# Seven products of quarter sums in place of eight quarter products: the up product of a two-layer hybrid model on one Trainium2 core

## The chip, the core and the metric

The kernel runs on one core of a Trainium2 chip. A core has a tensor engine (TensorE, in the profile PE for its matmuls and PEld for its weight loads), a vector engine (VectorE, DVE), a scalar engine (ScalarE, ACT), GpSimd (POOL) and SyncE (SP), which here issues nearly all transfers between DRAM and the on-chip memory SBUF. Each engine works its own list of instructions in order and waits on the others by semaphores; matmul results lie in PSUM, which DVE and ACT read. The metric is the device time of one execution in microseconds.

## What is computed

The model has two layers, width 1024, 1024 tokens, hidden width 2816, everything in float32. The change concerns the feed-forward part, `conv_ffn`, once in each layer:

```python
def rms_norm(x, gain):
    xf = x.astype(jnp.float32)
    y = xf * lax.rsqrt(jnp.mean(xf * xf, axis=-1, keepdims=True) + EPS)
    return (y * gain.astype(jnp.float32)).astype(x.dtype)

def conv_ffn(x, w_up, conv_w, conv_b, w_down):
    hid = causal_dwconv(x @ w_up, conv_w, conv_b)
    gate, val = jnp.split(hid, 2, axis=-1)
    return (jax.nn.gelu(gate) * val) @ w_down

def reference(...):
    for l in range(DEPTH):                        # DEPTH = 2
        h = rms_norm(x, g[0])
        if l % 2 == 0:
            ...                                   # recurrent mixers: hgrn2_mix and rglru_mix, then even_w_out
        else:
            ...                                   # fox_attention over 16 heads, then odd_w_out
        x = x + rms_norm(mix, g[1])
        h = rms_norm(x, g[2])
        x = x + rms_norm(conv_ffn(h, ffn_w_up[l], ffn_conv_w[l], ffn_conv_b[l], ffn_w_down[l]), g[3])
    return x
```

`x @ w_up` gives 2 × 2816 columns (gate and val), the convolution runs over three tokens of each column, and the gated product goes through `w_down`. In the terms of the kernel a column block of 128 is a *f* (22 of them, for gate and val), a block of 128 input channels is a *k* (8), and the tokens are two *halves* of 512.

## The kernel before

**Exact products.** A float32 operand is split in two: its leading 12 bits (a cast on ACT, L153 or L158) and the exact rest (a subtraction on DVE, L154 or L159; on POOL while `low[0]` is set). Each product of 128 × 128 by 128 × 512 is three matmuls, `mm3` (L161 to L164): lead by lead, lead by rest, rest by lead.

**Weights.** `load_split` fetches a piece of 128 × 512 by SP into one of three buffers (`rawp`, tile `raw`), casts it and subtracts. The split goes into one of four buffers `hl` (`wp`), or, for the pieces of `w_down` that half 1 keeps (`wk`), into room of its own. The raw buffer is free again when the subtraction is done.

**Up.** `ffn` runs over the halves, in each over f, in each over gate and val. `proj_cols` makes 8 k × 3 matmuls into a PSUM bank `pj`; ACT scales and adds the bias (L371), DVE adds the two earlier tokens out of PSUM (L376), with the last two columns of half 0 kept in `halo` (L381, L386); then gelu on ACT (L389), the product of gate and val on DVE (L390), and the split into the tile `act`, which stays in SBUF for down. So up of a half is followed by down of the same half, and `w_up` is fetched twice in each layer.

**Down and out.** `tok_proj` is a product with tokens on the PSUM partitions: for the first 512 output columns it goes over all k, in each fetching a weight piece and making 4 token tiles × 3 matmuls, then again for the second 512 columns (in passes over token tiles, `passes`). Half 1 of down has the callback `beside=keep`, which during the first columns also fetches and keeps the second columns' weights of the first 8 k (layer 0) or 16 k (layer 1). The norm of the result, the residual and the norm of the next stage follow on ACT and DVE (`squares` L296, `gains` L300, residual L338, `norm_rows` L230 and L236). The normed rows are transposed on PE and split (`turn`); `turn_later` sets after how many product steps that is done, by `NORM_STEPS`, so that other products stand between.

**Order.** PE's order is the order of the program (from layer 0's out product on it is fixed by hand); the lists of ACT, DVE, POOL and SP are set by a scheduler when the kernel is built. On all of them an instruction that waits holds up everything behind it.

## Time and profile before

Three runs took 2567.44 us in the median (2566.65 to 2569.66). The profiled execution has a span of 2567.0 us.

| | busy us | share | instructions |
|---|---|---|---|
| PE | 2489.4 | 97% | 11790 |
| DVE | 1658.2 | 65% | 3440 |
| ACT | 1190.4 | 46% | 2234 |
| POOL | 214.3 | 8% | 187 |

251.39 MB of transfers went at 98 GB/s in the mean. Up takes about 440 to 690 and 830 to 1070 us in layer 0, 1830 to 2080 and 2200 to 2440 us in layer 1; down follows each of them.

A row of a group reads: line, engine, operation, written tile<-read tiles, shapes, xcount | busy us, mean ns of one | idle us of the engine just before, and what ended most of it. A row of a timeline reads: start, duration, engine, line, operation, [idle before <-what released it]. A row of waits reads: who waits <- for whom: us in total, times, longest.

### The profile page before, as it was taken

To read this page: it belongs to the slowest core of one execution; us is meant where nothing else is said; L and a number is where in the kernel's file an instruction comes from. 1 tells how busy PE (TensorE), PEld (TensorE's weight loads), DVE (VectorE), ACT (ScalarE), POOL (GpSimd) and SP (SyncE) were. 2 spreads that over 40 slices of the span, in tenths; PEclk is the share of its full clock that TensorE was granted. 3 is DMA by queue.
4 is the path that set the end of the run, shared out by engine and by line. 5 is a ranking of instruction groups with operands and counts; after the bars stand their busy time and mean duration, and the time that the engine had idled before them with its cause. 6 is when DMAs were issued, how large, how long until landed. Compare 5 with 4: busy or idle time off the path is not lost.

```text
span 2567.0 us, 33472 instructions
## 1 busy us (share of the span) xinstructions
PE 2489.4 (97%) x11790; PEld 2050.7 (80%) x11790; DVE 1658.2 (65%) x3440; ACT 1190.4 (46%) x2234; POOL 214.3 (8%) x187
## 2 busy tenths in 40 slices
PE   8999999999999999999989999989899999999998
PEld 6887787788887788887778888877788888788887
DVE  5677766866524766636788888886766642666643
ACT  5333754544423444434556565664544432344441
POOL 2000001200001100000111111132300000300000
PEclk9999999999999999999999999999999999999999
DMA  4111125333334333335221222125433332533343
GB/s 133 33 42 34 47 90 181 124 96 98 99 97 138 98 96 97 125 110 162 69 51 45 53 56 52 51 89 188 159 91 98 96 99 99 156 99 95 101 160 112
DMA packets 131833, 251.39 MB, mean 98 GB/s; under 512 B 16112, under 2 KB 21520, under 8 KB 131664
## 3 DMA queue, kind: packets, MB, share of 16 engines
q1 hardware_dynamic: 129792, 244.34, 31.0%
q0 software_dynamic: 1440, 4.38, 0.7%
q8 instruction: 93, 1.52, 0.2%
q14 instruction: 76, 0.62, 0.1%
q10 hardware_dynamic: 432, 0.53, 0.1%
HBM read 219.23 MB, written 21.56 MB: 94 GB/s over the span
## 4 chain that ended last, share of the span: by engine, by line
PE 78%; DVE 14%; ACT 3%; DMA 2%; issue 2%; POOL 0%; SPq 0%; DVEq 0%; ACTq 0%; POOLq 0%
PE pj L162 15%; PE pj L163 15%; PE pj L164 15%; PE dn L162 7%; PE dn L163 7%; PE dn L164 7%; DVE nm L1003 2%; ACT pl L1013 2%; PE py L162 1%; DVE pt L159 1%; PE py L164 1%; PE py L163 1%; DVE lg L1001 1%; DVE y L338 1%; DVE ht L236 1%
## 5 line engine op out<-in xcount | busy, mean ns | idle before, releaser
L162 PE MATMUL pj<-hh,hl 128*128 128x512 f32 x1952 | 781.3, 400 | 18.1 <-DVE cv L381 9.2
L164 PE MATMUL pj<-hh,hl 128*128 128x512 f32 x1952 | 764.4, 392 | 0.9 <-POOL hl L154 0.8
L163 PE MATMUL pj<-hl,hl 128*128 128x512 f32 x1952 | 764.3, 392 | 0.0
L153 ACT CAST hl<-raw 128x512 fp32r<-128x512 f32 x687 | 423.5, 618 | 624.7 <-PE dn L164 319.8
L154 DVE TENSOR_TENSOR hl<-raw,hl 128x512 fp32r<-128x512 f32 x567 | 391.6, 692 | 371.5 <-ACT hl L153 371.0
L162 PEld LDWEIGHTS pj<-hh,hl 128*128 128x128 f32 x1952 | 368.9, 189 | 87.3 <-issue 20.1
L164 PEld LDWEIGHTS pj<-hh,hl 128*128 128x128 f32 x1952 | 368.0, 189 | 81.0 <-POOL hl L154 2.2
L376 DVE SCALAR_TENSOR_TENSOR cv<-pj,cw,cv 128x511 f32<-128x511 f32 x352 | 262.6, 746 | 251.3 <-ACT cv L371 251.3
L163 PEld LDWEIGHTS pj<-hl,hl 128*128 128x128 f32 x1952 | 369.3, 189 | 65.4 <-issue 0.2
L154 POOL TENSOR_TENSOR hl<-raw,hl 128x512 fp32r<-128x512 f32 x120 | 163.5, 1367 | 1244.2 <-ACT hl L153 1218.5
L371 ACT ACTIVATE cv<-pj,cw 128x512 f32<-128x512 f32 x176 | 137.3, 780 | 219.8 <-PE pj L164 219.6
L163 PE MATMUL dn<-hl,act 128*128 128x512 f32 x608 | 236.5, 389 | 0.0
L162 PE MATMUL dn<-hl,act 128*128 128x512 f32 x608 | 236.5, 389 | 0.0
L164 PE MATMUL dn<-hl,act 128*128 128x512 f32 x608 | 236.5, 389 | 0.0
L164 PEld LDWEIGHTS dn<-hl,act 128*128 128x128 f32 x608 | 114.1, 188 | 23.8
L162 PEld LDWEIGHTS dn<-hl,act 128*128 128x128 f32 x608 | 114.1, 188 | 23.6
L163 PEld LDWEIGHTS dn<-hl,act 128*128 128x128 f32 x608 | 114.1, 188 | 23.6
L158 ACT CAST pt<-tr 128x512 fp32r<-128x512 f32 (+1 forms) x160 | 86.8, 543 | 51.0 <-PE tr L1031 50.1
L1003 DVE TENSOR_REDUCE nm<-lg 128x1 f32<-128x512 f32 (+2 forms) x192 | 105.4, 553 | 4.6 <-PE lg L999 1.0
L159 DVE TENSOR_TENSOR pt<-tr,pt 128x512 fp32r<-128x512 f32 (+1 forms) x160 | 100.9, 633 | 7.9 <-ACT pt L158 6.3
L1013 ACT ACTIVATE pl<-lg,nm 128x512 f32<-128x512 f32 (+3 forms) x128 | 76.7, 605 | 43.9 <-DVE nm L1011 41.1
L1047 PE MATMUL o<-pt,v 128*128 128x256 f32 x320 | 77.5, 309 | 14.1 <-DVE pt L159 10.3
(323 smaller groups left out, 3354.4 us busy)
## 6 DMA issues: line engine op xcount, KB each, us to landing
raw<-in_w_up_dram SPq DMA_DIRECT2D x352, 256.0 KB
raw<-in_w_down_dram SPq DMA_DIRECT2D x202, 256.0 KB
raw<-in_w_out_dram SPq DMA_DIRECT2D x71, 256.0 KB
mid<-y SPq DMA_DIRECT2D x24, 512.0 KB
xt<-mid SPq DMA_DIRECT2D x24, 512.0 KB
raw<-in_w_qkv_dram SPq DMA_DIRECT2D x48, 256.0 KB
raw<-in_w_mix_dram SPq DMA_DIRECT2D x40, 256.0 KB
xr<-in_x_cols_dram SPq DMA_DIRECT2D x16, 256.0 KB
```

Source lines behind the costliest of these rows:

```text
L153: act.copy(hl[:, 0], raw)
L154: (pool if low[0] else dve).tensor_tensor(out=hl[:, 1], in0=raw, in1=hl[:, 0].bitcast(F32), op=ALU.subtract)
L158: act.copy(hi, src)
L159: dve.tensor_tensor(out=lo, in0=src, in1=hi.bitcast(F32), op=ALU.subtract)
L162: pe.matmul(o, wh, xh, start=start, stop=False)
L163: pe.matmul(o, wh, xl, start=False, stop=False)
L164: pe.matmul(o, wl, xh, start=False, stop=stop)
L371: act.activation(out=y, in_=u, func=AF.Identity, scale=cw[:, 2, c : c + 1], bias=cw[:, 3, c : c + 1])
L376: dve.scalar_tensor_tensor(out=y[:, d:], in0=u[:, : HT - d], scalar=wcol, in1=y[:, d:], op0=ALU.mult, op1=ALU.add,)
L1003: dve.tensor_reduce(out=nm[:, x0 : x0 + 1], in_=lg[:, :n], axis=AX.X, op=ALU.max, negate=True)
L1013: act.activation(out=p[:, cs], in_=lg[:, :n], func=AF.Exp, bias=nm[:, 0:1], accum_out=sm[:, x0 : x0 + 1])
L1047: pe.matmul(o, v[:, kb, :], pt[s][:, 0:256], start=(u == 0 and s == 0), stop=False, skip_group_check=True,)
```

## The change

The up product of both halves is made as a two-by-two block product in the form of Strassen and Winograd. With the weights as blocks a11, a12 (gate; the two halves of the input channels) and a21, a22 (val), and the activations as b11, b21 (half 0) and b12, b22 (half 1), the four results need seven products of quarter size:

- P1 = a11·b11, a12·b21, s2·t2, s1·t1, s3·t3, s4·b22, a22·t4;
- s1 = a21 + a22, s2 = s1 − a11, s3 = a11 − a21, s4 = a12 − s2;
- t1 = b12 − b11, t2 = b22 − t1, t3 = b22 − b12, t4 = the difference of b21 and t2.

Each is 4 k × 3 matmuls. `up(l, hb)` holds the whole stage for both halves:

- The normed rows are now only copied after the transpose, in float32 (`hb`, one tile per half); the sums are formed in float32 and then split. Half 0's b11 and b21 are split first.
- For the first three f (`AHEAD`) the two products P1 and a12·b21 need half 0 alone. They are made while half 1 is still being normed and turned, and their sums are written to DRAM (`started`) and fetched back in the loop.
- The operands t2, t1, t3, b22, t4 are then formed and split: the differences on DVE and POOL, the splits on ACT and DVE (t4's rest on POOL).
- In the loop over f POOL and DVE form s1 to s4, the splits follow; the products add up in two PSUM banks `y` and `z`, with copies of P1, u2 and q kept in SBUF (`tap`). The sums c1 (gate) and c2 (val) lie in SBUF over all 1024 tokens, so that the convolution runs over 1024 at once without `halo`.
- The gated product of a f, 512 KB, is written to DRAM (`hidden`). Down fetches it again, 128 × 512 for each k of each half, through the raw ring, casts and subtracts (`fetch`, up to three k ahead).
- `w_up` is fetched once in each layer. The pools are opened by stage (`open_stage`, `open_rows`). Layer 0's out product of half 1 runs its second columns in two passes of two token tiles; `NORM_STEPS` of half 1 is (27, 20) in place of (36, 46). A gain vector of layer 1 is loaded when first used.

```diff
--- before.py
+++ after.py
...
-NORM_STEPS, DOWN_NORM_STEPS, TURN_STEPS = (36, 46), (32, 42), 2
+NORM_STEPS, DOWN_NORM_STEPS, TURN_STEPS = ((36, 46), (27, 20)), (32, 42), 2
+AHEAD = 3
...
+    pools = {}
+    stage = [None]
+    def open_stage(**bufs):
+        if stage[0] is not None:
+            stage[0].close()
+        stage[0] = ExitStack()
+        pools.clear()
+        for name, n in bufs.items():
+            pools[name] = stage[0].enter_context(tc.tile_pool(name=name, bufs=n, reuse_waits="tile"))
+    def open_rows():
+        open_stage(s4=NSLOT, s2=NHALF)
+    open_rows()
...
+    hidden = [
+        [dram.tile([P, T], F32, tag=f"hid{l}_{f}", name=f"hid{l}_{f}") for f in range(FT)]
+        for l in range(2)
+    ]
+    started = [dram.tile([P, 2, HT], F32, tag=f"started{f}", name=f"started{f}") for f in range(AHEAD)]
...
-            hh, hl = h[t // 4]
             c0 = (t % 4) * P
             tp = tr()
             for k in range(4):
                 pe.transpose(tp[:, k, :], ht[:, (4 * q + k) * P : (4 * q + k + 1) * P], ident)
+            if not isinstance(h[t // 4], tuple):
+                act.copy(h[t // 4][:, 4 * q : 4 * q + 4, c0 : c0 + P], tp)
+                return
+            hh, hl = h[t // 4]
             split(hh[:, 4 * q : 4 * q + 4, c0 : c0 + P], hl[:, 4 * q : 4 * q + 4, c0 : c0 + P], tp)
...
-        turn_later(ts, hts, h, NORM_STEPS[ts[0] // 2 % 2])
+        turn_later(ts, hts, h, NORM_STEPS[ts[0] // 4][ts[0] // 2 % 2])
...
+    def combined(raws, begun):
+        a11, a12, a21, a22 = raws
+        def split_of(src, eng):
+            w = wp.tile([P, 2, 4, P], F32R, tag="hl", name="hl")
+            act.copy(w[:, 0], src)
+            eng.tensor_tensor(out=w[:, 1], in0=src, in1=w[:, 0].bitcast(F32), op=ALU.subtract)
+            return w
+        def mixed(eng, a, b, op):
+            t = pools["ws"].tile([P, 4, P], F32, tag="ws", name="ws")
+            eng.tensor_tensor(out=t, in0=a, in1=b, op=op)
+            return t
+        s1 = mixed(pool, a21, a22, ALU.add)
+        if not begun:
+            yield split_of(a11, pool)
+            yield split_of(a12, pool)
+        s2 = mixed(dve, s1, a11, ALU.subtract)
+        yield split_of(s2, dve)
+        yield split_of(s1, dve)
+        s3 = mixed(pool, a11, a21, ALU.subtract)
+        yield split_of(s3, dve)
+        s4 = mixed(dve, a12, s2, ALU.subtract)
+        yield split_of(s4, dve)
+        yield split_of(a22, dve)
+    def up(l, hb):
+        cw = cws[l]
+        def operand(own):
+            shape = [P, 2, 4, HT]
+            if own:
+                return pools["ops"].tile(shape, F32R, tag="ops", name="op")
+            return hpool.tile(shape, F32R, tag="hT", name="op")
+        def split_k(b, k, src, eng):
+            act.copy(b[:, 0, k], src)
+            eng.tensor_tensor(out=b[:, 1, k], in0=src, in1=b[:, 0, k].bitcast(F32), op=ALU.subtract)
+        def raw(f, s, i):
+            own = s == 0 and "uraw" in pools
+            name = "uraw" if own else "raw"
+            t = (pools["uraw"] if own else rawp).tile([P, 4, P], F32, tag=name, name=name)
+            nc.sync.dma_start(out=t, in_=w_up[l, s * FT + f, i].rearrange("p (k c) -> p k c", k=4))
+            return t
+        def tap(name="tap"):
+            return pools["tap"].tile([P, HT], F32, tag="tap", name=name)
+        def room(name):
+            return pools["cc" if name == "c" else "cy"].tile([P, T], F32, tag=name, name=name)
+        def product(o, a, b, start):
+            for k in range(4):
+                mm3(o, a[:, 0, k], a[:, 1, k], b[:, 0, k], b[:, 1, k], start and k == 0, k == 3, True)
+                run_later()
+        def conv(s, f, c):
+            ch = s * FT + f
+            y = room("y")
+            act.activation(out=y, in_=c, func=AF.Identity, scale=cw[:, 2, ch : ch + 1], bias=cw[:, 3, ch : ch + 1])
+            for d in (1, 2):
+                dve.scalar_tensor_tensor(
+                    out=y[:, d:], in0=c[:, : T - d], scalar=cw[:, 2 - d, ch : ch + 1], in1=y[:, d:],
+                    op0=ALU.mult, op1=ALU.add,
+                )
+            return y
+        b11, b21 = operand(False), operand(False)
+        for k in range(4):
+            split_k(b11, k, hb[0][:, k], dve)
+        for k in range(4):
+            split_k(b21, k, hb[0][:, 4 + k], dve)
+        first = [slice(0, HT), slice(HT, T)]
+        for f in range(AHEAD):
+            ws = []
+            for i in range(2):
+                a = raw(f, 0, i)
+                w = wp.tile([P, 2, 4, P], F32R, tag="hl", name="hl")
+                act.copy(w[:, 0], a)
+                pool.tensor_tensor(out=w[:, 1], in0=a, in1=w[:, 0].bitcast(F32), op=ALU.subtract)
+                ws.append(w)
+            y, x = pj(), bank("x")
+            product(y, ws[0], b11, True)
+            p1, c1 = half_slot("p1"), half_slot("c1")
+            act.copy(p1, y)
+            product(x, ws[1], b21, True)
+            dve.tensor_tensor(out=c1, in0=x, in1=p1, op=ALU.add)
+            nc.sync.dma_start(out=started[f][:, 0], in_=p1)
+            nc.sync.dma_start(out=started[f][:, 1], in_=c1)
+        run_later(True)
+        open_stage(ops=4, uraw=5, ws=3, tap=5, cc=4, cy=2)
+        t2, t1, t3, b22 = (operand(True) for _ in range(4))
+        t4 = operand(False)
+        for k in range(4):
+            h11, h21, h12, h22 = hb[0][:, k], hb[0][:, 4 + k], hb[1][:, k], hb[1][:, 4 + k]
+            dve.tensor_tensor(out=h11, in0=h12, in1=h11, op=ALU.subtract)
+            m = pools["ws"].tile([P, HT], F32, tag="ws", name="m")
+            dve.tensor_tensor(out=m, in0=h22, in1=h11, op=ALU.subtract)
+            split_k(t2, k, m, dve)
+            pool.tensor_tensor(out=h21, in0=h21, in1=m, op=ALU.subtract)
+        for k in range(4):
+            split_k(t1, k, hb[0][:, k], dve)
+        for k in range(4):
+            h12, h22 = hb[1][:, k], hb[1][:, 4 + k]
+            pool.tensor_tensor(out=h12, in0=h22, in1=h12, op=ALU.subtract)
+            split_k(t3, k, h12, dve)
+        for k in range(4):
+            split_k(b22, k, hb[1][:, 4 + k], dve)
+        for k in range(4):
+            split_k(t4, k, hb[0][:, 4 + k], pool)
+        for f in range(FT):
+            raws = [raw(f, s, i) for s in range(2) for i in range(2)]
+            ws = combined(raws, f < AHEAD)
+            y = pj()
+            c1 = room("c")
+            if f < AHEAD:
+                p1 = tap("p1")
+                nc.sync.dma_start(out=p1, in_=started[f][:, 0])
+                nc.sync.dma_start(out=c1[:, first[0]], in_=started[f][:, 1])
+            else:
+                p1 = None
+                product(y, next(ws), b11, True)
+                p1_ = tap("p1")
+                act.copy(p1_, y)
+                x = bank("x")
+                product(x, next(ws), b21, True)
+                dve.tensor_tensor(out=c1[:, first[0]], in0=x, in1=p1_, op=ALU.add)
+            product(y, next(ws), t2, p1 is not None)
+            u2, q = tap("u2"), tap("q")
+            if p1 is None:
+                act.copy(u2, y)
+            else:
+                dve.tensor_tensor(out=u2, in0=y, in1=p1, op=ALU.add)
+            z = bank("z")
+            product(z, next(ws), t1, True)
+            if p1 is None:
+                act.copy(q, z)
+            else:
+                dve.tensor_tensor(out=q, in0=z, in1=p1, op=ALU.add)
+            product(y, next(ws), t3, False)
+            c2 = room("c")
+            dve.tensor_tensor(out=c2[:, first[1]], in0=y, in1=q, op=ALU.add)
+            product(z, next(ws), b22, False)
+            dve.tensor_tensor(out=c1[:, first[1]], in0=z, in1=u2, op=ALU.add)
+            gt = conv(0, f, c1)
+            act.activation(out=gt, in_=gt, func=AF.Gelu_apprx_tanh)
+            product(y, next(ws), t4, False)
+            if p1 is None:
+                act.copy(c2[:, first[0]], y)
+            else:
+                dve.tensor_tensor(out=c2[:, first[0]], in0=y, in1=p1, op=ALU.add)
+            vl = conv(1, f, c2)
+            dve.tensor_tensor(out=gt, in0=gt, in1=vl, op=ALU.mult)
+            nc.sync.dma_start(out=hidden[l][f], in_=gt)
+        open_rows()
+    def ffn(l, hb, xsrc, dst, tail, primed=None):
+        up(l, hb)
         gpost = gain_bcast(l, 3)
...
         for half in range(NH):
...
+            acts = [None] * FT
+            def fetch(k):
+                for f in range(k, min(k + 3, FT)):
+                    if acts[f] is None:
+                        r = rawp.tile([P, HT], F32, tag="raw", name="ar")
+                        nc.sync.dma_start(out=r, in_=hidden[l][f][:, half * HT : (half + 1) * HT])
+                        acts[f] = slot("act", (P, 2, HT), F32R)
+                        split(acts[f][:, 0], acts[f][:, 1], r)
             wsrc = lambda k, nh: w_down[l, k * P : (k + 1) * P, nh * HT : (nh + 1) * HT].unsqueeze(1)
             if half == 0:
...
+                tok_proj(half, acts, wsrc, xsrc, gpost, dst, tail, True, beside=fetch)
                 continue
             nroom = 4 if l else 2
             room = [hpool.tile([P, 4, 2, 1, HT], F32R, tag="hT", name="wk") for _ in range(nroom)]
             kept = {}
             def keep(k):
+                fetch(k)
                 if k < 4 * nroom:
                     kept[k] = load_split(wsrc(k, 1), 1, lambda shape: room[k // 4][:, k % 4])
             tok_proj(half, acts, wsrc, xsrc, gpost, dst, tail, l == 0, passes=PASSES[l], beside=keep, kept=kept, primed=primed)
...
-    h2 = new_h()
+    h2 = rows_cols()
...
-            x_rows, gpost, mids[0], tail, half == 0,
+            x_rows, gpost, mids[0], tail, half == 0, passes=PASSES[0] if half else ((0, 1, 2, 3),),
...
-    h4 = new_h()
+    h4 = rows_cols()
...
```

**The order, at three places.** In the rows below line numbers of the changed kernel are its own: L425 is the subtraction of an operand's split (`op`), L484 and L486 are t1 and t2 (`m`), L390 and L395 a weight's rest and mix, L168 a weight piece's load, L543 the write of a hidden tile, L557 the fetch of a hidden piece (`ar`); hb_2781 and hb_2782 are the two halves of layer 0's rows.

DVE at the start of layer 0's up stage, before. Half 1's last norm and first frames of half 0 alternate:

```order
L376 SCALAR_TENSOR_TENSOR cv<-pj,cw_116,cv 128x511
L129 SCALAR_TENSOR_TENSOR rc_m<-rc_m,ss 128x2
L376 SCALAR_TENSOR_TENSOR cv<-pj,cw_116,cv 128x510
L130 SCALAR_TENSOR_TENSOR ry_m<-rc_m,ry_m 128x2
L386 COPY halo<-pj 128x2
L338 SCALAR_TENSOR_TENSOR y_3553<-y_3297,ry_m,xt 128x512
L338 SCALAR_TENSOR_TENSOR y_3553<-y_3553,ry_m,xt 128x512
```

And now, from the third parked sum on:

```order
L475 TENSOR_TENSOR c_3865<-x,p_3864 128x512
L484 TENSOR_TENSOR hb_2781<-hb_2782,hb_2781 128x512 x2
L486 TENSOR_TENSOR m<-hb_2782,hb_2781 128x512 x2
L484 TENSOR_TENSOR hb_2781<-hb_2782,hb_2781 128x512
L425 TENSOR_TENSOR op<-m,op 128x512 x2
L486 TENSOR_TENSOR m<-hb_2782,hb_2781 128x512
...
L425 TENSOR_TENSOR op<-hb_2781,op 128x512
L425 TENSOR_TENSOR op<-hb_2782,op 128x512 x8
L395 TENSOR_TENSOR ws<-ws,uraw 128x512
L390 TENSOR_TENSOR hl<-ws,hl 128x512 x3
L395 TENSOR_TENSOR ws<-uraw,ws 128x512
```

All operand operations of the stage stand in one stretch ahead of the first frame's weights s2 (the first L395) and its split.

SP at the end of layer 0's up stage, now. Before, the list held only loads of weight pieces there:

```order
L543 DMA hid0_19_124<-y_6805 128x1024
L168 DMA raw_7148<-in_w_down_dram 128x512
L557 DMA ar_7153<-hid0_0_105 128x512
L543 DMA hid0_20_125<-y_6952 128x1024
L557 DMA ar_7158<-hid0_1_106 128x512
L557 DMA ar_7163<-hid0_2_107 128x512
L543 DMA hid0_21_126<-y_7099 128x1024
L168 DMA raw_7180<-in_w_down_dram 128x512
L557 DMA ar_7185<-hid0_3_108 128x512
```

The second weight piece of down stands behind the write of the last hidden tile.

SP around half 1 of layer 0's down, before:

```order
L304 DMA xt<-mid_3_84 128x1024
L148 DMA raw<-in_w_up_dram 128x512 x6
L345 DMA mid_2_91<-y_6340 128x1024
L345 DMA mid_3_92<-y_6342 128x1024
L148 DMA raw<-in_w_up_dram 128x512 x76
L148 DMA raw<-in_w_down_dram 128x512 x51
```

And now, from the second k's weight on:

```order
L168 DMA raw_8158<-in_w_down_dram 128x512
L168 DMA raw_8174<-in_w_down_dram 128x512
L557 DMA ar_8179<-hid0_3_108 128x512
L168 DMA raw_8184<-in_w_down_dram 128x512
L372 DMA mid1_2_91<-y1_8026 128x1024
L372 DMA mid1_3_92<-y1_8028 128x1024
L168 DMA raw_8200<-in_w_down_dram 128x512
L557 DMA ar_8205<-hid0_4_109 128x512
L168 DMA raw_8210<-in_w_down_dram 128x512
```

Half 0's norm no longer has an up stage behind it, and each k of half 1 has three loads through the ring in place of two.

More of the change, by code (lines that the diff above doesn't have):

```diff
@@ L159, in split, with mm3 @@
         dve.tensor_tensor(out=lo, in0=src, in1=hi.bitcast(F32), op=ALU.subtract)
-    def mm3(o, wh, wl, xh, xl, start, stop):
-        pe.matmul(o, wh, xh, start=start, stop=False)
-        pe.matmul(o, wh, xl, start=False, stop=False)
-        pe.matmul(o, wl, xh, start=False, stop=stop)
+    def mm3(o, wh, wl, xh, xl, start, stop, taps=False):
+        pe.matmul(o, wh, xh, start=start, stop=False, skip_group_check=taps)
+        pe.matmul(o, wh, xl, start=False, stop=False, skip_group_check=taps)
+        pe.matmul(o, wl, xh, start=False, stop=stop, skip_group_check=taps)
     def load_cols(w, alloc=None):
@@ L186, in new_h, with rows_cols @@
         return [new_half(i) for i in range(NH)]
+    def rows_cols():
+        return [hpool.tile([P, KT, HT], F32, tag="hT", name=f"hb{i}") for i in range(NH)]
     def gain_bcast(l, i):
@@ L354, in tail_to @@
         return lambda ts, xts, _: pre_norm(ts, xts, g, hn)
-    def ffn(l, h, xsrc, dst, tail, primed=None):
+    def combined(raws, begun):
[21 more added lines that the diff above has]
+        yield split_of(a22, dve)
@@ L358, in ffn @@
+    def ffn(l, hb, xsrc, dst, tail, primed=None):
+        up(l, hb)
         gpost = gain_bcast(l, 3)
-        cw = cws[l]
         for half in range(NH):
-            acts = []
-            for f in range(FT):
-                low[0] = f < 4
-                conv = []
-                for s in range(2):
-                    c = s * FT + f
-                    wt = load_cols(w_up[l, c])
-                    u = pj()
-                    proj_cols(u, wt, h, half)
-                    y = half_slot("cv")
-                    act.activation(
-                        out=y, in_=u, func=AF.Identity, scale=cw[:, 2, c : c + 1], bias=cw[:, 3, c : c + 1]
-                    )
-                    for d in (1, 2):
-                        wcol = cw[:, 2 - d, c : c + 1]
-                        dve.scalar_tensor_tensor(
-                            out=y[:, d:], in0=u[:, : HT - d], scalar=wcol, in1=y[:, d:],
-                            op0=ALU.mult, op1=ALU.add,
-                        )
-                        if half:
-                            dve.scalar_tensor_tensor(
-                                out=y[:, :d], in0=halo[:, c, 2 - d :], scalar=wcol, in1=y[:, :d],
-                                op0=ALU.mult, op1=ALU.add,
-                            )
-                    if not half:
-                        dve.tensor_copy(halo[:, c, :], u[:, HT - 2 :])
-                    conv.append(y)
-                gt, vl = conv
-                act.activation(out=gt, in_=gt, func=AF.Gelu_apprx_tanh)
-                dve.tensor_tensor(out=gt, in0=gt, in1=vl, op=ALU.mult)
-                a = slot("act", (P, 2, HT), F32R)
-                split(a[:, 0], a[:, 1], gt)
-                acts.append(a)
@@ L395, in ffn @@
             if half == 0:
-                tok_proj(half, acts, wsrc, xsrc, gpost, dst, tail, True)
+                tok_proj(half, acts, wsrc, xsrc, gpost, dst, tail, True, beside=fetch)
                 continue
@@ L417, in hybrid_kernel @@
     fb = const.tile([16, 1], F32, name="fb")
-    halo = const.tile([P, 2 * FT, 2], F32, name="halo")
     rh = const.tile([P, 4, 3], F32, name="rh")
@@ L1138, in hybrid_kernel @@
     first = project(0, [(nm, half) for half in range(NH) for nm in "qkv"])
-    g3 = gain_bcast(1, 0)
+    g3 = []
     def tail_attention(ts, xts, spare):
+        if not g3:
+            g3.extend(gain_bcast(1, 0))
         hts = norm_rows(xts, g3, spare)
@@ L1209, in hybrid_kernel @@
     manual.close()
+    stage[0].close()
 _INS = [
```

12 lines of the change are left out of this document (5 added, 7 removed).

## The prediction

> **What bounds the kernel now.** I read the page's totals and its chain first, then the groups, then single stretches.
>
> ```profile
> span 2567.0 us, 33472 instructions
> PE 2489.4 (97%) x11790; PEld 2050.7 (80%) x11790; DVE 1658.2 (65%) x3440; ACT 1190.4 (46%) x2234; POOL 214.3 (8%) x187
> PE 78%; DVE 14%; ACT 3%; DMA 2%; issue 2%; POOL 0%; SPq 0%; DVEq 0%; ACTq 0%; POOLq 0%
> L162 PE MATMUL pj<-hh,hl 128*128 128x512 f32 x1952 | 781.3, 400 | 18.1 <-DVE cv L381 9.2
> ```
>
> TensorE (PE) is busy 97% of the span and is 78% of the chain. Its largest group, three lines of 1952 products into `pj`, waited 18.1 us in all. So a product taken away is time gained, as long as whatever feeds PE keeps its cover. The other engines have room on average (DVE 65%, ACT 46%); what follows asks where they don't. The price of a product is its pitch, not its 400 ns, since products overlap. The windows view has it (length, then busy time and count for PE, PEld, DVE, ACT, POOL; clock; DMA share; GB/s):
>
> ```profile
> 690.00:812.00 122.00, 122.00 (x540) 101.06 (x539) 35.51 (x54) 33.19 (x58) 3.18 (x3) 1.00 0.31 97
> 2446.00:2486.00 40.00, 40.00 (x179) 33.10 (x178) 19.28 (x28) 17.27 (x28) 0.00 (x0) 1.00 0.57 183
> ```
>
> 540 products in 122.00 us at full clock are 0.226 us each. A down step of one k (four token tiles by three products) is 12 × 0.226 = 2.71 us.
>
> **Step 1, the products.** For each layer, f and the pair gate/val, eight products of 4 k × 3 matmuls become seven: 12 fewer per f, 22 × 2 × 12 = 528 in all. 528 × 0.226 = **-119.3 us**, if nothing else changes. A round of f lasts 7 × 12 × 0.226 = 19.0 us of PE.
>
> **Step 2, the loop over f.** Its other work per f is priced from these rows:
>
> ```profile
> L153 ACT CAST hl<-raw 128x512 fp32r<-128x512 f32 x687 | 423.5, 618 | 624.7 <-PE dn L164 319.8
> L154 DVE TENSOR_TENSOR hl<-raw,hl 128x512 fp32r<-128x512 f32 x567 | 391.6, 692 | 371.5 <-ACT hl L153 371.0
> L376 DVE SCALAR_TENSOR_TENSOR cv<-pj,cw,cv 128x511 f32<-128x511 f32 x352 | 262.6, 746 | 251.3 <-ACT cv L371 251.3
> L371 ACT ACTIVATE cv<-pj,cw 128x512 f32<-128x512 f32 x176 | 137.3, 780 | 219.8 <-PE pj L164 219.6
> L389 ACT ACTIVATE cv<-cv 128x512 f32<-128x512 f32 x88 | 55.5, 630 | 61.8 <-DVE cv L381 58.8 <-DVE ry_m L123 1.5 <-DVE halo L386 1.3
> ```
>
> DVE has ten operations of 512 columns (five splits, two weight mixes, three sums), 10 × 0.69 = 6.9, and five of 1024 (four taps, the product of gate and val), at most 5 × 2 × 0.746 = 7.5: 14.4 of 19.0 us. ACT has seven casts, four copies and three wide ones: 11 × 0.62 + 2 × 1.56 + 1.26 = 11.2 us. Both fit behind PE. POOL adds four per f. The tightest place is the copy of P1 on ACT: PE may not add t2's product on top until it is done, and it can stand behind the gelu of the f before. From the order that leaves about 1.3 us of room. I take **0**, with 38 rounds without parked sums × 1 us = +38 as the upper bound.
>
> **Step 3, the start of the up stage.** The 24 operand operations on DVE (four differences, four mixes, sixteen splits for t2, t1, t3, b22) need the second half's turned rows, and the first left operand PE still lacks (s2 and its split) stands behind them in DVE's queue. Until then PE has only the parked products, 3 × 24 × 0.226 = 16.3 us. At the same time POOL does eight operations on the same tiles and s1, s3. How DVE and POOL share is in the timeline (start, duration, operation, count):
>
> ```profile
> 409.56 2.07 DVE L236 SCALAR_TENSOR_TENSOR ht<-y,ry_m,gain 128x512 f32<-128x512 f32 x3
> 439.70 1.30 POOL L154 TENSOR_TENSOR hl<-raw,hl 128x512 fp32r<-128x512 f32 x1 [1.44 <-ACT hl L153]
> 454.19 5.83 DVE L236 SCALAR_TENSOR_TENSOR ht<-y,ry_m,gain 128x512 f32<-128x512 f32 x4
> 454.26 6.88 POOL L154 TENSOR_TENSOR hl<-raw,hl 128x512 fp32r<-128x512 f32 x4 [7.79 <-ACT hl L153]
> ```
>
> Alone, DVE needs 0.69 us for one and POOL 1.30; side by side four took 5.83 and 6.88, so a pair costs 1.72. Ten such pairs are 17.2 us, and the 16 other operations of the 26 up to s2's split 16 × 0.69 = 11.0: 28.2, with the first cast and a wait between engines about 30 us. Without POOL in the way it would be 26 × 0.69 = 17.9, the lower bound; I take 30, because all these operations have both inputs in SBUF, as those in the row.
>
> The Trainium skill ("SBUF — State Buffer", Who interferes with whom) says that a VectorE instruction with two SBUF inputs contends with a GpSimd instruction that reads SBUF, and that the loser blocks for the whole instruction. By that rule the sum would be 26 × 0.69 + 10 × 1.30 = 30.9 us, by the averages of the rows without contention 17.9; the row at 454.19 agrees with the rule.
>
> When do the turned rows come? The chain of before shows the norm after the out product of layer 0's second half:
>
> ```profile
> 441.39 3.85 DMA xt<-in_x_dram
> 445.35 2.34 DVE y L338 x2
> 454.24 5.78 DVE ht L236 x4
> 472.96 3.77 DVE ht L236 x4
> ```
>
> The product ends at 441.39, the first pair of tiles is normed at 460.02 and the second at 476.73, 35 us after. Before hid that behind half 0's up products (these rows' stretch also holds their convolutions); after has the parked 16.3 us. Layer 0's two passes bring the first pair forward by 2 × 3 × 8 × 0.226 = 10.9 us, so that turns and parked work run on to about the last turn and PE then idles the 30 us: with 2.6 for the gap between the passes, 3 in the parked products, 2.6 of slow clock, 3 in the three frames that take their sums back, and less the 6 us that before lost here (the row at 462.88 and slow products after it), **+35**. These rows show PE's gaps, and the slow clock behind them:
>
> ```profile
> 462.88 0.47 PE L162 MATMUL pj<-hh,hl 128*128 128x512 f32 x1 [4.14 <-DVE halo L386]
> 837.20 0.77 PE L162 MATMUL pj<-hh,hl 128*128 128x512 f32 x1 [7.54 <-DVE cv L381]
> 838.19 0.63 PE L164 MATMUL pj<-hh,hl 128*128 128x512 f32 x1
> 838.62 0.63 PE L162 MATMUL pj<-hh,hl 128*128 128x512 f32 x1
> 1847.02 0.77 PE L162 MATMUL pj<-hh,hl 128*128 128x512 f32 x1 [4.17 <-DVE halo L386]
> 2210.12 0.47 PE L162 MATMUL pj<-hh,hl 128*128 128x512 f32 x1 [1.71 <-DVE cv L381]
> ```
>
> After a gap products come every 0.43 us, about a dozen of them: 12 × 0.2 = 2.4 to 2.6 us. Layer 1 keeps one pass of four tiles, so both pairs are normed after the product. I take 29 us for that (35 less the 6 us of convolution work in the stretch), 3 for the last turns and 30 for the operands: 62 us after the product, less PE's 16.3 us and some 4 us of turns, 41.7, plus 2.6 and 3, less the 4.6 that before lost at 1847.02: **+43**. Bounds for the two together: 78 as taken, 54 without POOL in the way.
>
> **Step 4, up to down.** The first hidden tile is cast and split behind f = 21's gelu on ACT and its product on DVE: copy 0.62, scale 1.56, two taps 3.0, product 1.4, split 0.69 are at most 7.3 us after up's last product, with twice the price of 512 columns for each wide one; I take 6, since its fixed part comes once (0 if it came early). The second weight piece stands on SP behind the write of the last hidden tile, which waits for that product; then a load, a cast and a split. A load takes, in the chain,
>
> ```profile
> 1174.69 2.66 DMA raw<-in_w_down_dram
> 1178.82 2.50 DMA raw<-in_w_down_dram
> ```
>
> so it is there 5.4 (6 less the split and a little) + 2.66 + 0.62 + 0.69 + about 1 = 10.4 us after up's end, where PE has 2.71 us to do: 7.6 lost, plus 2 from the ring (next step): **+9.5 a layer, +19** (bounds 0 and 24).
>
> **Step 5, three loads through three buffers.** In down's first product every load passes the same ring. What one costs when the ring is the limit is in the window 2446 to 2486 above: 28 casts in 40 us, 1.43 us each. Its waits say that it is the limit:
>
> ```profile
> SPq L148 <- DVE hl L154: 16.3, 16, 1.4
> SPq L148 <- DVE wk L154: 11.9, 12, 1.3
> ACT wk L153 <- DMA raw<-in_w_down_dram: 9.5, 12, 1.3
> ACT hl L153 <- DMA raw<-in_w_down_dram: 8.7, 10, 1.5
> ```
>
> SP waited 28 of 40 us for a split to free a buffer, and ACT waited 18 for the data. In half 1 of after, a k needs a weight, a kept weight and a hidden piece: 3 × 1.43 = 4.29 us against 2.71 of products, a loss of 1.58 a k, while kept weights come (8 k in layer 0, 16 in layer 1); with two loads 2.86, 0.15 a k. Up stood between the halves before; now half 0's norm stands ahead of half 1's first pieces on ACT and DVE, so that in layer 0 k = 0 starts about 9.5 us after half 0's end and k = 3 only after 29.9: 29.9 - 3 × 2.71 = 21.8, plus 5 × 1.58 and 14 × 0.15, is 31.8; less the 7.54 and 2.6 lost before at 837.20: **+21.5**. In layer 1 (no norm for a next stage) k = 1 starts after 14.4: 11.7 + 14 × 1.58 + 1 = 34.8, less 2.5: **+32**. If the ring kept pace with PE and the pieces came first, +10 would be left of the two together; that is the lower bound.
>
> **The sum.** -119.3 + 0 + 35 + 43 + 19 + 21.5 + 32 = **+31**: 2567.0 + 31 = **2598 us**. The profiled 2567.0 lies within 0.02% of the median 2567.44, so nothing is added for it.
>
> **Rivals.**
> *The covers hold (faster).* POOL and DVE don't meet (24 less in step 3), the ring follows PE, and the norm lets the first pieces through (43 less in step 5): 2598 - 24 - 43 = 2531; with one of the two, 2555 to 2574. For it: in 2446 to 2486 PE was busy all 40.00 us in spite of two loads a k. Against it: the ring had a lead to live on there, and three loads were never tried. It wins if the losses of steps 3 to 5 stay under 119 of the 150 taken. I give it 2540 as its middle.
>
> *The loop stalls (slower still).* If the copy of P1, or DVE held by POOL, comes 1 us late in each of 38 rounds, 2598 + 38 = 2636. For it: four POOL operations a round, each of which can add 1.1 us to a DVE operation (14.4 + 4.4 = 18.8 of 19.0). Against it: sums from PSUM have one SBUF input only, and the rows show pairs with two. It decides from the point where one round lasts longer than 19.0 us.
>
> *No saving at all.* That the change would not remove the products is ruled out: PE's list is shorter by the matmuls of step 1.
>
> **How the numbers follow.** The sum 0.58 (its own range 2574 to 2620, half of steps 3 and 5's bounds either way), the covers hold 0.26, the loop stalls 0.16. The prediction is 2598 us; the range 2540 to 2638 leaves out the lower half of the second case and the end of the third. 0.2% (5 us) is about what a measurement of this kernel tells from no change. Faster: the second case and a little of the first, 0.27; within 0.2%: 0.06; slower: 0.67.
>
> **What would show it.** Windows over an up stage: 19.0 us a round and PE at 100% confirm steps 1 and 2. PE's idle time after the last turn of hb (about 30 and 42 us), released by the split of s2, confirms step 3, with DVE's operand rows near 1.7 us where POOL runs. In down's second half PE's steps of 4.3 us, with ACT waiting for DMA and SP for a split, confirm step 5; steps of 2.71 would make it wrong, and so would a first left operand that is ready within 18 us.

## The result

The changed kernel takes 2600.55 us in the median of four runs (2598.77 to 2601.87), the kernel before beside it 2567.05 (2565.36 to 2569.66): a ratio of 1.0132 with a 95% interval of 1.0117 to 1.0146. It is slower by 33 us; the prediction was 2598. The profiled execution has a span of 2599.4 us, 32.4 more than before's 2567.0, and the differences below are taken between these two.

The page of the kernel after, with the totals, the chain by engine and the groups that answer to those shown of before (columns as there):

```profile
span 2599.4 us, 32334 instructions
PE 2410.4 (93%) x11262; PEld 1957.8 (75%) x11262; DVE 1781.0 (69%) x3166; ACT 1253.6 (48%) x2280; POOL 502.6 (19%) x323
PE 64%; DVE 18%; DMA 8%; ACT 6%; issue 3%; POOL 1%; SPq 0%; ACTq 0%; DVEq 0%; POOLq 0%
L182 PE MATMUL pj<-op,hl 128*128 128x512 f32 x704 | 277.2, 394 | 57.7 <-ACT hl L389 55.8
L182 PE MATMUL dn<-hl,act 128*128 128x512 f32 x608 | 247.2, 407 | 39.2 <-ACT hl L173 20.9
L395 POOL TENSOR_TENSOR ws<-raw 128x512 f32<-128x512 f32 x44 | 151.8, 3451 | 307.7 <-DVE ws L395 264.2
L390 DVE TENSOR_TENSOR hl<-ws,hl 128x512 fp32r<-128x512 f32 x176 | 143.3, 818 | 4.9 <-ACT hl L389 4.6
```

PE has 11262 instructions in place of 11790, 528 fewer, as the change says. But its share of the chain fell from 78% to 64%. Two groups of products wait where they did not: the first product of an up stage's loop, 55.8 us for a left operand's cast (L389), and down's products, 39.2 us before L182 alone, for weights and hidden pieces. In the kernel before, all the products into `pj` waited 18.1 us together, and down's products not at all:

```profile
L162 PE MATMUL dn<-hl,act 128*128 128x512 f32 x608 | 236.5, 389 | 0.0
```

The windows view, in order of time, shows where (length, then busy time and count of PE, PEld, DVE, ACT, POOL; clock; DMA share; GB/s):

```profile
455.00:493.00 38.00, 9.21 (x42) 7.44 (x43) 32.94 (x43) 16.83 (x32) 20.21 (x13) 0.65 0.34 112
530.00:898.00 368.00, 368.00 (x1626) 304.80 (x1625) 270.19 (x293) 181.04 (x266) 150.33 (x76) 1.00 0.25 82
1044.00:1085.00 41.00, 29.93 (x95) 20.47 (x94) 26.06 (x54) 16.41 (x27) 0.00 (x0) 0.84 0.60 186
1853.00:1889.00 36.00, 8.01 (x43) 6.21 (x42) 27.97 (x29) 16.38 (x30) 18.48 (x12) 0.64 0.22 73
2440.00:2510.00 70.00, 52.37 (x179) 34.57 (x179) 32.75 (x48) 28.28 (x46) 0.00 (x0) 0.94 0.61 188
```

In the loop PE is busy all 368 us, 1626 records at 0.226 us: the saving is there in full. In the two starts (455 and 1853) PE has 9 of 38 and 8 of 36 us, while DVE is busy for 33 and 28. In the two second halves of down (1044 and 2440) PE works 30 of 41 and 52 of 70 us, part of it at a lower clock (0.84 and 0.94), and no other engine is near its limit either.

From the start times of PE's products, less what the same products and transposes take at full pace (0.227 and 0.09 us each), follows the time lost in each stage:

| place | lost before | lost after | more | predicted |
|---|---|---|---|---|
| 528 products at 0.227 us | | | -119.7 | -119.3 |
| loop over f, from its fourth frame | 0 | -0.4 | 0 | 0 |
| start of up, layer 0 | 9.6 | 37.8 | +28.2 | +35 |
| start of up, layer 1 | 9.6 | 45.6 | +36.0 | +43 |
| up to down, both layers | 0 | 14.8 + 14.0 | +28.8 | +19 |
| down's halves, layer 0 | 11.1 | 30.5 | +19.4 | +21.5 |
| down's halves, layer 1 | 2.2 | 41.5 | +39.3 | +32 |
| sum | | | +32.0 | +31 |

### The profile page after: what moved, and what is told of

It reads as the page before. It is cut to its first block, busy times and chain, and to the rows that moved or that the text cites. A ratio compares the mean times of both kernels' runs of the same rounds, so it can differ in the third digit from the quotient of the medians.

```text
span 2599.4 us, 32334 instructions
## 1 busy us (share of the span) xinstructions
PE 2410.4 (93%) x11262; PEld 1957.8 (75%) x11262; DVE 1781.0 (69%) x3166; ACT 1253.6 (48%) x2280; POOL 502.6 (19%) x323
## 4 chain that ended last, share of the span: by engine, by line
PE 64%; DVE 18%; DMA 8%; ACT 6%; issue 3%; POOL 1%; SPq 0%; ACTq 0%; DVEq 0%; POOLq 0%
PE pj L182 9%; PE pj L183 9%; PE pj L184 9%; PE dn L182 5%; PE dn L183 5%; PE dn L184 5%; DMA raw<-in_w_down_dram 5%; PE z L184 3%; PE z L183 3%; PE z L182 3%; DVE nm L1170 2%; ACT pl L1180 2%; DMA ar<-hid 2%; DVE pt L179 2%; PE py L182 1%
## 5 line engine op out<-in xcount | busy, mean ns | idle before, releaser
L174 DVE TENSOR_TENSOR hl<-raw,hl 128x512 fp32r<-128x512 f32 x287 | 198.3, 694 | 291.7 <-ACT hl L173 291.3
L173 ACT CAST hl<-raw 128x512 fp32r<-128x512 f32 x343 | 212.3, 621 | 374.7 <-PE dn L184 191.5
L182 PE MATMUL pj<-op,hl 128*128 128x512 f32 x704 | 277.2, 394 | 57.7 <-ACT hl L389 55.8
L182 PE MATMUL dn<-hl,act 128*128 128x512 f32 x608 | 247.2, 407 | 39.2 <-ACT hl L173 20.9
L184 PE MATMUL pj<-op,hl 128*128 128x512 f32 x704 | 276.4, 393 | 0.5 <-POOL hl L468 0.5
L183 PE MATMUL pj<-op,hl 128*128 128x512 f32 x704 | 276.0, 392 | 0.0
L450 DVE SCALAR_TENSOR_TENSOR y<-c,cw,y 128x1023 f32<-128x1023 f32 (+1 forms) x176 | 226.9, 1290 | 28.6 <-ACT y L448 27.2
L182 PE MATMUL pj<-hh,hl 128*128 128x512 f32 x544 | 228.6, 420 | 0.2 <-DVE offs L1017 0.2
L183 PE MATMUL pj<-hl,hl 128*128 128x512 f32 x544 | 213.7, 393 | 0.0
L184 PE MATMUL pj<-hh,hl 128*128 128x512 f32 x544 | 213.7, 393 | 0.0
L395 POOL TENSOR_TENSOR ws<-raw 128x512 f32<-128x512 f32 x44 | 151.8, 3451 | 307.7 <-DVE ws L395 264.2
L182 PEld LDWEIGHTS pj<-op,hl 128*128 128x128 f32 x704 | 133.5, 190 | 87.8 <-ACT hl L389 58.1
L389 ACT CAST hl<-ws 128x512 fp32r<-128x512 f32 x176 | 109.3, 623 | 163.4 <-PE z L184 93.7
L182 PEld LDWEIGHTS dn<-hl,act 128*128 128x128 f32 x608 | 117.8, 194 | 77.5 <-ACT hl L173 32.6
L184 PEld LDWEIGHTS pj<-op,hl 128*128 128x128 f32 x704 | 133.4, 189 | 29.8 <-DVE hl L390 1.1
L183 PEld LDWEIGHTS pj<-op,hl 128*128 128x128 f32 x704 | 133.6, 190 | 27.6
L390 DVE TENSOR_TENSOR hl<-ws,hl 128x512 fp32r<-128x512 f32 x176 | 143.3, 818 | 4.9 <-ACT hl L389 4.6
```

The lines of the kernel that those rows point to most:

```text
L173: act.copy(hl[:, 0], raw)
L174: (pool if low[0] else dve).tensor_tensor(out=hl[:, 1], in0=raw, in1=hl[:, 0].bitcast(F32), op=ALU.subtract)
L182: pe.matmul(o, wh, xh, start=start, stop=False, skip_group_check=taps)
L183: pe.matmul(o, wh, xl, start=False, stop=False, skip_group_check=taps)
L184: pe.matmul(o, wl, xh, start=False, stop=stop, skip_group_check=taps)
L389: act.copy(w[:, 0], src)
```

## The experiments

Each kernel is the changed one with the edit shown; the rest is as it was. Times are medians, to be set against 2600.55 of the change and 2567 to 2570 of the kernel before beside them.

**e1: the first frame's left operands first.**

```diff
+        w0 = weights(0)                      # combined(...) of frame 0
+        early = [next(w0) for _ in range(2)] # s2 and s1 split, ahead of t2 ... t4
         for k in range(4):
             h11, h21, h12, h22 = ...
```

> The first frame's two left operands (s2, s1) are formed and split ahead of the operands t2 to t4; nothing else changes. If PE's 28 us of idle time at the start of each up stage come from s2 standing last in DVE's queue, PE can begin t2's products as soon as t2 itself is split; its last piece is now about the 22nd of 27 operations, so idle falls from 28 to about 20 us: 15 us less for both layers (2585). If the operands themselves gate it (t2's last split late in any order), the change is under 5 us (2596 to 2600).

2598.36 us. PE's row at the start of layer 0's loop in the change, then PE's rows there in e1:

```profile
492.63 0.80 PE L182 MATMUL pj<-op,hl 128*128 128x512 f32 x1 [28.25 <-ACT hl L389]
```

```profile
476.65 0.80 PE L183 MATMUL pj<-op,hl 128*128 128x512 f32 x1 [8.90 <-ACT op L425]
478.89 0.79 PE L184 MATMUL pj<-op,hl 128*128 128x512 f32 x1 [1.45 <-DVE op L426]
483.45 0.79 PE L184 MATMUL pj<-op,hl 128*128 128x512 f32 x1 [2.51 <-DVE op L426]
489.22 0.79 PE L184 MATMUL pj<-op,hl 128*128 128x512 f32 x1 [2.52 <-DVE op L426]
```

PE begins at 476.65 in place of 492.63, and then waits for one operand piece after the other. The long wait was cut up, not shortened: layer 0's stage takes as long (460.0 us from its first to its last product, 459.6 in the change), and layer 1's is 1.9 us shorter (465.5 from 467.4). So s2's place in the queue was what the trace named, but not the cause; DVE's work is.

**e2: no POOL among the operands.**

```diff
-            pool.tensor_tensor(out=h21, in0=h21, in1=m, op=ALU.subtract)
+            dve.tensor_tensor(out=h21, in0=h21, in1=m, op=ALU.subtract)
 ...
-            pool.tensor_tensor(out=h12, in0=h22, in1=h12, op=ALU.subtract)
+            dve.tensor_tensor(out=h12, in0=h22, in1=h12, op=ALU.subtract)
```

> The eight operand differences of each layer that POOL made are made by DVE. If POOL and DVE exclude each other (a pair 1.7 us), DVE alone needs 34 x 0.65 = 22 us for what took 28 in the two layers: 4 to 6 us less a layer, 2589 to 2592. If POOL worked beside DVE, eight more operations are in DVE's way: 8 x 0.65 = 5 us more a layer, 2610.

2589.85 us, 10.7 less, with eight operations more on DVE in each layer. The timelines of the change (DVE, then POOL) and of e2 (DVE, then PE):

```profile
465.81 3.43 DVE L486 TENSOR_TENSOR m<-hb,hb 128x512 f32<-128x512 f32 x2
474.79 0.68 DVE L484 TENSOR_TENSOR hb<-hb,hb 128x512 f32<-128x512 f32 x1
475.39 1.75 DVE L425 TENSOR_TENSOR op<-hb,op 128x512 fp32r<-128x512 f32 x1
465.44 3.25 POOL L493 TENSOR_TENSOR hb<-hb 128x512 f32<-128x512 f32 x2 [8.08 <-DVE hb L484]
```

```profile
465.47 1.29 DVE L486 TENSOR_TENSOR m<-hb,hb 128x512 f32<-128x512 f32 x2
488.60 0.79 PE L182 MATMUL pj<-op,hl 128*128 128x512 f32 x1 [24.56 <-ACT hl L389]
```

Two operations take 3.43 us while POOL runs two, and 1.29 without: the pair of 1.72 us of the prediction. The Trainium skill ("SBUF — State Buffer", Who interferes with whom) states the exclusion. These rows agree that the two wait for each other; but a pair costs 1.72 us, less than the 0.69 and 1.30 of the two alone in sequence. A POOL operation beside it here costs a DVE operation about 1.0 us.

**e3: the hidden pieces outside the raw ring.** They land in the second half of their own tile and are subtracted in place; transfers and bytes are the same.

```diff
-                        r = rawp.tile([P, HT], F32, tag="raw", name="ar")
-                        nc.sync.dma_start(out=r, in_=hidden[l][f][...])
                         acts[f] = slot("act", (P, 2, HT), F32R)
+                        r = acts[f][:, 1].bitcast(F32)
+                        nc.sync.dma_start(out=r, in_=hidden[l][f][...])
                         split(acts[f][:, 0], acts[f][:, 1], r)
```

> The hidden pieces are fetched straight into the rest's half of their own tile and subtracted in place, so that the three raw buffers carry weights alone; bytes and transfers are the same. If the three buffers set the pace of down (three loads a k at 1.4 us each), the steps of half 1 fall from 4.1 towards 2.9 us: 8 x 1.2 in layer 0 and 16 x 1.2 in layer 1, with a little at the heads, 30 us less (2570). If DRAM or the transfers themselves set the pace, steps stay at 4.1 us and the time within 5 us of 2600.

2559.82 us, 40.7 less and by itself below the kernel before (ratio 0.9963, interval 0.995 to 0.9975). Half 1 of down in the two layers: first layer 1's stretch from 2430 us in the change (layer 0's is above), then both stretches in e3:

```profile
2430.00:2510.00 80.00, 55.29 (x185) 36.67 (x186) 41.67 (x82) 29.97 (x51) 0.00 (x0) 0.90 0.59 185
```

```profile
1044.00:1085.00 41.00, 38.15 (x172) 30.48 (x171) 33.36 (x64) 26.45 (x47) 0.00 (x0) 0.95 0.76 249
2430.00:2510.00 80.00, 80.00 (x346) 65.95 (x345) 40.80 (x64) 37.20 (x65) 0.00 (x0) 0.97 0.56 181
```

In layer 1 PE works all 80 us and makes 346 products in place of 185, and in layer 0 the transfers run at 249 in place of 186 GB/s. DRAM was not the limit; the three buffers were. What is left are the heads: PE waits 17.44 us at half 1's first product of layer 1. SP's queue there (start, time, issues):

```profile
2412.26 1.98 SPq L331 DMA_DIRECT2D xt<-mid  x4
2419.05 4.31 SPq L372 DMA_DIRECT2D out_dram<-y  x4
2423.45 3.93 SPq L558 DMA_DIRECT2D act<-hid  x7
2428.83 0.79 PE L182 MATMUL dn<-hl,act 128*128 128x512 f32 x1 [17.44 <-ACT act L178]
```

The fetches of half 1 stand behind four writes of half 0's results, which wait for the norm. In the change itself the first three pieces had been fetched ahead of these writes (see step 5 below); the long heads of 14.0 and 17.4 us are e3's own.

**e4: eight parked frames** (`AHEAD = 8`).

> Eight frames in place of three have their first two products made early and parked: 5 x 24 x 0.227 = 27 us more of PE work beside the norm and the operands, in each layer; the products in all are the same. If the start of up is lack of work for PE, its idle time of 31 (layer 0) and 39 us (layer 1) falls by 27 each, less some 3 for five more frames that take sums back: 50 us less, 2550. If the early products' own work on DVE, POOL and ACT delays the norm and the operands as much as it covers, or the parked sums' transfers stall the loop, less than 20 us is gained (2580 or more).

2591.48 us, 9 less: the case of less than 20. The wait of 28 us at the loop's first product is gone, but up to that product 20.3 and 29.8 us are lost in the two layers (34.2 and 41.7 in the change), and in the eight frames after it 14.6 and 14.1, in short waits; see e11.

**e5: e3 with earlier fetches.**

```diff
+                def ahead(k):                 # called in half 0's second product
+                    if 0 < k <= 8:
+                        fetch(k - 1, 1, 1)    # one piece of half 1
+                fetch(0, 3)                   # half 0's first three, ahead of the first weight
```

> As e3_in_place, and the hidden pieces are fetched earlier: half 0's first three ahead of down's first weight, half 1's first eight during half 0's second product, so that on SP they no longer stand behind the writes of half 0's results. If the heads of the two halves (7, 14, 8 and 18 us of idle PE in e3) come from that place in SP's queue, those of half 1 fall to 1 to 2 us and those of half 0 to some 3: 35 to 40 us less than e3, about 2523. If the first pieces wait for their tiles' memory or for ACT and DVE behind the norm, less than 12 us is gained (2548 or more).

2541.67 us, 18 less than e3. Half 1's heads fell from 14.0 and 17.4 us to 1.3 and 1.0, so SP's queue was their cause. Half 0's stayed at 7.0 and 7.3. The program asks for their pieces first, but in SP's list they still stand behind three weights, whose issue took 6.9 us:

```profile
896.81 6.91 SPq L168 DMA_DIRECT2D raw<-in_w_down_dram  x3
903.77 0.90 SPq L562 DMA_DIRECT2D act<-hid  x2
907.19 1.29 ACT L178 CAST act<-act 128x512 fp32r<-128x512 f32 x2 [3.13 <-DMA act<-hid]
```

Behind the heads of half 1, about 10 us a layer are lost between its fifth and its seventeenth k, so the gain was half of what was expected. The trace of e5 shows half of that in layer 1 at the same place in SP's queue. The four writes now hold up the next weights, and PE waits 2.71 us for such a cast before the sixth k:

```profile
2409.47 4.31 SPq L374 DMA_DIRECT2D out_dram<-y  x4
2413.88 1.76 SPq L168 DMA_DIRECT2D raw<-in_w_down_dram  x3
2417.89 0.62 ACT L173 CAST hl<-raw 128x512 fp32r<-128x512 f32 x1 [6.76 <-DMA raw<-in_w_down_dram]
```

No run takes the writes out of the weights' way, so what that is worth stays open.

**e6: layer 1's out product in two passes**, as layer 0 has it (`passes=PASSES[0] if half else ((0, 1, 2, 3),)`).

> Only layer 1's out product of half 1 is changed: its second columns in two passes of two token tiles, as layer 0 has it. If layer 1's up waits for the norm of all four tiles (10.6 us ahead of the last turns in the trace), the first pair is normed 10.9 us earlier for 2.6 us at the passes' border: 6 to 8 us less, 2593. If DVE's work of norm and operands together is the bound, it only moves the idle time: within 3 us of 2600.

2599.17 us. Layer 1's up stage became 8 us shorter (459.5 from 467.4), as the first case had it, and the out product ahead of it 5 us longer (53.2 from 48.3, up to the first product of up); the time shows 1.4 us of the 3 that are left. So the number is that of the backlog case, but the mechanism is only in part: the earlier norm did shorten the up stage, and the two passes cost most of it.

**e7: the start's edits together** (e1, e2, `AHEAD = 5`, and the parked frames' rests on DVE instead of POOL).

> Three edits at the start of up together: POOL's operand differences on DVE (e2), the first frame's left operands first (e1), five parked frames in place of three, their left operands' rests on DVE and not on POOL. If cover and the exclusion of POOL and DVE add up, 11 + 2 x 10.9 us less: 2567 to 2570. If all of it is one backlog of DVE, which parked frames add to (their sums are DVE's: in e4 27 us of cover a layer brought 2 to 3), it stays at e2's gain and little more: 2583 to 2590.

2588.22 us: 1.6 us more than e2's own gain.

**e8 and e9: what helped, together.** e8 is e5 with e1 and e2, and with half 0's first four hidden pieces fetched and split during up's last frames:

```diff
+            if f == FT - 3:
+                pre = hpool.tile([P, 4, 2, HT], F32R, tag="hT", name="pre")
+                for i in range(4):
+                    r = pre[:, i, 1].bitcast(F32)
+                    nc.sync.dma_start(out=r, in_=hidden[l][i][:, 0:HT])
+                    split(pre[:, i, 0], pre[:, i, 1], r)
```

> e5 with POOL's operand differences on DVE (e2) and the first frame's left operands first (e1); in addition half 0's first four hidden pieces are fetched and split during up's last frames, into the operand pool's free tile, so that their casts stand ahead of the last gelu on ACT. If the terms are separate places on PE's path they add up: 2541.7 less 11 (e2) and 2 x 7 (the heads of half 0 in e5, 7.4 and 7.7 us) is 2517. If the heads only move on to the second weight piece or the fifth hidden piece, the pre-split brings under 5 us: 2526 to 2531.

> e8 with five parked frames in place of three, their left operands' rests on DVE. If up's start is one backlog of DVE, as e4 and e7 say (e7 beat e2 by 1.6 us), nothing or 2 us is gained on e8: 2515 to 2518. If the cover counts once POOL is out of the way, 2 x 10.9 = 22 us at most are gained: 2495 to 2505.

2524.85 and 2516.54 us. In both the step from up to down has no loss at all: what e3, e5 and this edit change, the way of the first hidden pieces and of the loads around them, removes the whole 14 to 15 us of each layer. The window of e8 around that step in layer 0:

```profile
895.00:915.00 20.00, 20.00 (x89) 16.54 (x89) 14.74 (x20) 11.06 (x17) 1.59 (x3) 1.00 0.65 204
```

e8 missed its sum by 8 us, because its up stages are no shorter than the change's (458.8 and 469.2 us, against 455.9 and 463.3 in e2): beside e2, e1 costs what e2 gains. e9 lies in its first case (2515 to 2518), but by luck: that case allowed 2 us of gain on a sum that e8 had missed, and e9 gained 8.3. So two more parked frames, with their rests on DVE, are worth more than nothing and less than half of their 22 us.

**e11: is it DVE's backlog?** e4 with less work for DVE. It leaves the convolution's two earlier taps out for the first ten frames of each layer.

```diff
-            for d in (1, 2):
+            for d in (1, 2) if f >= 10 else ():
```

> e4 (eight parked frames), and the first ten frames of each layer leave the convolution's two earlier taps out, which takes 40 wide operations, 40 x 1.29 = 52 us of DVE's time, out of the start of each up stage and nothing from PE, POOL or the transfers. If e4's 27 us of cover a layer were eaten by a backlog of DVE, the stalls of the first frames go and the cover comes through: about 2 x 20 us under e4, 2545 to 2560. If transfers, POOL or ACT ate it, the time stays within 8 us of e4: 2583 to 2591.

2572.54 us, 18.9 less than e4, between the two expectations. The windows of e4, then of e11, from 495 us on:

```profile
495.00:530.00 35.00, 28.31 (x109) 21.08 (x107) 23.97 (x32) 13.69 (x20) 15.20 (x11) 0.90 0.43 142
530.00:565.00 35.00, 33.85 (x147) 27.43 (x148) 33.46 (x41) 13.44 (x18) 8.51 (x5) 1.00 0.44 148
565.00:600.00 35.00, 33.25 (x139) 26.72 (x138) 32.04 (x40) 15.58 (x21) 7.45 (x4) 0.95 0.42 146
```

```profile
495.00:530.00 35.00, 27.98 (x113) 21.49 (x112) 22.74 (x31) 14.90 (x22) 15.06 (x11) 0.95 0.44 152
530.00:565.00 35.00, 35.00 (x156) 28.97 (x155) 25.49 (x34) 17.84 (x22) 6.95 (x5) 1.00 0.51 162
565.00:600.00 35.00, 35.00 (x156) 29.01 (x155) 26.61 (x33) 15.16 (x20) 6.46 (x5) 1.00 0.51 167
```

From 530 us on the waits are gone once DVE falls from 33 to 26 us of 35: that half is DVE's backlog. Over the stage, the eight frames lose 3.5 and 3.3 us in place of 14.6 and 14.1, while the loss ahead of them stays (18.6 and 30.8 against 20.3 and 29.8). With three parked frames the edit was not run; it had little to win there, for the change loses 3.8 us in layer 0's first three frames and nothing after them. From 495 to 530 nothing changed, with DVE at 23 to 24 of 35. There, in the trace, parked products wait for rests made by POOL (L468) and casts on ACT. That these, and not a third thing, are the rest of e4's missing gain was not tested alone.

**e10 and e12: the last versions.** e10 is e9 without e1; e12 is e10 with e6.

> e9 without the early left operands of the first frame (e1). If the start is a backlog of DVE, an earlier first product of PE is worth nothing, and putting s2 and s1 ahead only delays operands: 4 to 9 us less than e9, 2508 to 2513. If the early first product is worth what e1 showed on its own, 2 us are lost: 2519.

> e10 with layer 1's out product of half 1 in two passes of two tiles (e6). If the norm of the second pair, 11 us of PE's wait in e9's layer 1, is still on the path, the 10.9 us it comes earlier count now that POOL is out of the way: 4 to 8 us less than e10. If DVE's backlog is all, nothing is gained or the passes' border costs 3 to 5 us, as in e6.

2510.13 and 2502.27 us; e12 has a ratio of 0.9745 to the kernel before (interval 0.9731 to 0.976), 67 us faster than before and 98 faster than the change. e10's 6.4 us are what an early first product costs; and e6, worth nothing in the change, is worth 8 us here. In the profiled executions, which differ by only 1.7 us, layer 1's up stage is 13.5 us shorter (449.0 from 462.5) and the out product 6 us longer. Why the up stage gains more here than in the change was not tested.

## Why the prediction came out

The total was right to 2 us, and each step had its sign. That it was so close is luck: the steps were off by -7, -7, +10, -2 and +7 us, and these errors cancelled. The range given to the sum is also narrower than its words: half of 24 and half of 43 either way would be 2564 to 2632, not 2574 to 2620.

- **Step 1** (products, -119.3) and **step 2** (the loop, 0): right. The rival of a stalling loop is out. POOL and DVE do collide in it (the group rows above have 818 ns for a split that takes 0.69 alone, and 3451 for POOL's sum of 1.30), but the loop had the room: 368.00 of 368.00 us.
- **Step 3** (start, 35 and 43): the mechanism held, both terms were 7 us too large (28.2 and 36.0). The idle time itself was near, and made up as counted: in layer 0 DVE runs 25 operations without a pause from 464.60 to 490.45 us, ten of them of 1.74 to 1.76 us beside POOL and fifteen of 0.68 to 0.69, and the cast of s2 follows. It was 28.25 us of an expected 30 in layer 0, and in layer 1 two waits that sum to 38.2 of 41.7:

```profile
1852.21 1.09 PE L273 MATMUL tr<-ident,ht 128*128 128x128 f32 x4 [10.65 <-DVE ht L260]
1888.76 0.80 PE L182 MATMUL pj<-op,hl 128*128 128x512 f32 x1 [27.56 <-ACT hl L389]
```

  Of the 7 us in layer 0, the idle time makes 1.8, what I added around it (passes' gap, parked products, three frames: 8.6 us, where this stretch has some 7) 1.6, and what I took off for before 3.6: 9.6 us were lost there in each layer, not 6 and 4.6. One of the signs was badly chosen: that a first left operand ready early would show step 3 wrong. e1 had it 16 us earlier and gained 2 us, since the operands themselves fill DVE. The lower bound of 18 us without POOL was not reached by any run: in e2 POOL's eight operations are DVE's, and the wait was 24.56 us.
- **Step 4** (up to down, 9.5 a layer): 14.8 and 14.0. The head was as described: the cast follows the gelu, and the second weight is issued behind the last hidden tile's write.

```profile
901.27 1.06 ACT L535 ACTIVATE y<-y 128x1024 f32<-128x1024 f32 x1
902.23 1.64 ACT L178 CAST act<-ar 128x512 fp32r<-128x512 f32 x3
905.13 0.32 SPq L543 DMA_DIRECT2D hid<-y  x1
905.74 0.33 SPq L168 DMA_DIRECT2D raw<-in_w_down_dram  x1
```

  By the first product of the second k 8 us were lost in each layer, of 7.6 taken. Mis-sized was the ring's part, 2 us: some 6 more are lost in small pieces over the other k of down's first product, and with the ring relieved (e3) 9.2 and 9.9 us remained of 14.8 and 14.0.
- **Step 5** (halves, 21.5 and 32): 19.4 and 39.3. The ring was the main cause (e3: -40.7 in all), with 4.29 us a k in layer 1 (five steps from 2467.75 to 2489.20), as estimated, and 4.49 over the fourteen k from the second on. The late start was as the step says too: in layer 0 half 0's norm stands ahead of the first pieces' casts on ACT, and k = 0 starts 8.2 us after half 0's end and k = 3 after 28.1 (9.5 and 29.9 taken); in layer 1 PE waits 6.37 us in k = 0 for a subtraction that stands behind the norm on DVE, and k = 1 starts after 15.4 (14.4 taken).

```profile
1038.71 1.06 ACT L254 ACTIVATE xt<-y 128x1024 f32<-128x1024 f32 x1 [4.24 <-DVE y L365]
1041.09 1.64 ACT L178 CAST act<-ar 128x512 fp32r<-128x512 f32 x3
1041.75 0.80 PE L182 MATMUL dn<-hl,act 128*128 128x512 f32 x1 [8.00 <-ACT act L178]
2434.53 2.98 SPq L372 DMA_DIRECT2D out_dram<-y  x3
2443.28 0.62 ACT L173 CAST wk<-raw 128x512 fp32r<-128x512 f32 x1 [11.59 <-DMA raw<-in_w_down_dram]
```

  What the step left out is SP's queue: the next weights are issued behind the writes of half 0's results, which wait for that norm (the last two rows, in layer 1), and in e3 the hidden pieces are. Mis-sized by 7 us was layer 1's term, most of it in the k behind the first: 14 × 1.58 + 1 = 23.1 taken, 28.7 measured. How much of that is the queue and how much the ring was not told apart.
- **The covers hold** was the rival with 0.26. Neither of its two parts held in the change; e3 is what the kernel would have been with one of them, and it is faster than before, as that rival's point of decision (losses under 119 of 150) says.

## What to carry to other kernels

A saving on the busiest engine is worth what the stages around it leave of it: here 120 us of products were won and 152 lost at six borders, and removing the border losses, not the product, decided the sign. When a stage is put through memory, count its transfers per step against the buffers they pass, and look where its fetches stand in the queue behind writes that wait. A wait that the trace names at the end of a queue may be the whole queue's work: bring the named one forward only if what stands before it is not needed at once.

## What was not expected of the hardware

- POOL and DVE side by side do less than DVE alone on these operations: with the eight differences on DVE as well (e2) PE's wait in layer 0 was 3.7 us shorter (24.56 against 28.25 us) than with them on POOL.
- Cover can cost what it covers: five more parked frames are 27 us of PE work a layer and shortened the up stages by 3.0 and 1.8 us (e4). 19 of the 45 us that were missing came back when DVE was relieved (e11).
